# MLP's first product by seven block products in a phase of its own, its result by way of DRAM: a fused S5 and MLP layer on one core

## The chip, the cores and the metric

The kernel runs on 1 core of one Trainium2 chip. The metric is the time of the program on the device in microseconds, the median of several runs. TensorE (PE) multiplies and writes to PSUM, which has 8 banks of 128x512 float32; VectorE (DVE), ScalarE (ACT) and GpSimd (POOL) work element by element; SyncE (SP) only issues transfers. SBUF holds 128 partitions.

## The reference

One layer over 1024 latent tokens of width 1024, with a short context. A diagonal state-space mixer (S5) comes first, then a squared-ReLU MLP of width 4096, each behind a modulated RMS norm:

```python
def _mlp(h, w1, b1, w2, b2):
    a = jax.nn.relu(h @ w1 + b1)
    return (a * a) @ w2 + b2
...
x = x + g1 * y            # y: S5, GELU, then z * sigmoid(z @ glu_w + glu_b)
x = x + g2 * _mlp(_modulate(_rmsnorm(x, norm2_g[i]), sh2, sc2),
                  mlp_w1[i], mlp_b1[i], mlp_w2[i], mlp_b2[i])
...
return _rmsnorm(x, final_g)
```

All is float32: w1 is 1024 x 4096, w2 4096 x 1024.

## The kernel before

Activations are held transposed: channels on partitions (8 tiles of 128, index `d` or `k`), tokens along the row, in two halves of 512 (`halves[0]`, `halves[1]`, index `hf`). A float32 operand of a product is split into a high half, which the format of TensorE holds exactly, and a low half, what is left of it. ACT makes the high half by a cast, DVE or POOL subtracts it from the source. `mm3` then multiplies high by high, high by low and low by high: three matmuls of 128x128 weights with a 128x512 operand.

The kernel has a fixed order: `tc.manual_schedule()` leaves every engine's instructions in the order in which the code names them, and each engine takes them one after the other. Waits between engines are put in where data demand them.

The stages that matter here come last. The S5 part ends at about 370 us. Then follows the gate `z @ glu_w` (matmuls of `gate`, results of `gate_out`): sigmoid on ACT, two operations on DVE, into the residual `acc`. `z_sum` on POOL adds the two halves of z again. `sum_sq` collects the sum of squares of `acc`, `norm_cols` and `norm_rows` turn it into a factor per token by small matmuls, and `norm2` writes the normalised and modulated activations, split, over z (`zt(k)`). This is done for the first half of the tokens, then for the second.

The MLP runs over 16 blocks `b` of 256 hidden units. Block b takes the columns 256b to 256b+255 of w1 (1 MB, `load_w1`) and the same rows of w2 (1 MB, `load_w2`). For each block and token half, `m1_` makes two hidden tiles `f` of 128 (24 matmuls each, over 8 `k`), relu and square on ACT, split into the tiles A or GW. `m2_` multiplies them by w2 (48 matmuls), and DVE adds each of the 8 results, times g2, to `acc` (L1089). Nothing between the two products leaves SBUF. The list `order` sets the turn of blocks and halves: `m1_` of one entry stands ahead of `m2_` of the entry before. The weights of the next block are split behind that (`next_w1`, `next_w2`), into regions of the tile W that alternate. Raw weights have two buffers, w1 in UT from block 2 on and w2 in T.

The last block's second half is cut into two pieces of 256 tokens, so that the final norm of the first half and the stores run beside it.

Of the kernel before, what the change touches and what calls it, by code (L numbers as in the profile page):

```python
# [47 lines left out]
def kernel(ctx, tc, cst, bc, x, xl, ada_w, glu_w, w1, w2, out):  # L48
# [16 lines left out]
    KD = dp.tile([8, 128 * 1024], F32, name="KD")  # L65

# [823 lines left out]
    ring = [[sb(10240 + 512 * i, 512) for i in range(3)] + [at(UT, 512 * i, 512) for i in range(4)]]  # L890
    nt = [0]

    def tmp():
        nt[0] += 1
        return ring[0][nt[0] % len(ring[0])]
# [9 lines left out]
    def wpart(i):  # L905
        return at(W, 4096 * i, 4096)

    def raw1(b):
        return vw(raw[b > 1], 8, 256)

    def load_w1(b):
        SP.dma_start(out=raw1(b), in_=w1.rearrange("(k p) f -> p k f", p=128)[:, :, 256 * b:256 * b + 256])

    def load_w2(b):
        SP.dma_start(out=vw(raw[0], 2, 1024), in_=w2.rearrange("(k p) f -> p k f", p=128)[:, 2 * b:2 * b + 2])

    def w1s(b):
        return vw(wpart((3, 1)[b % 2]), 2, 8, 256)

    def w2s(b):  # L920
        return vw(wpart((0, 2)[b % 2]), 2, 2, 1024)

    def split_w1(b):
        split(w1s(b)[:, 0], w1s(b)[:, 1], raw1(b))

    def split_w2(b, eng=V):
        split(w2s(b)[:, 0], w2s(b)[:, 1], vw(raw[0], 2, 1024), eng)
# [92 lines left out]
    load_w1(0)  # L1020
# [10 lines left out]
    split_w1(0)  # L1031
    load_w1(1)
# [7 lines left out]
    for d, b in ((4, 6), (5, 7), (6, 1), (7, 3)):  # L1040
        for k in range(8):
            gate(bank(b), d, 1, k)
            if (d, k) == (4, 1):
                rb = norm_rows(r_, 2)
                for _ in norm2(range(8), 0, rb):
                    pass
                for e in range(2):
                    sum_sq(e, halves[1])
    gate_outs([(2, 4), (3, 5), (4, 6), (5, 7)], 1)
    w1_hi, w1_lo = w1s(1)[:, 0], w1s(1)[:, 1]  # L1050
    S.copy(w1_hi, raw1(1))
    gate_outs([(6, 1), (7, 3)], 1)
    V.tensor_tensor(w1_lo, raw1(1), w1_hi.bitcast(F32), op=OP.subtract)  # L1053
    load_w2(0)


    na = [0]

    def m1_mm(b, f, hf, ks=range(8)):
        o = bank((2, 0, 1, 3)[na[0] % 4])  # L1060
        w, fs = w1s(b), slice(128 * f, 128 * f + 128)
        for k in ks:
            z = zt(k)
            mm3(o, (w[:, 0, k, fs], w[:, 1, k, fs]), (z[:, 0, halves[hf]], z[:, 1, halves[hf]]), k == 0, k == 7)
        return o

    def m1_(b, f, hf):
        return m1_out(b, f, m1_mm(b, f, hf))

    def m1_out(b, f, o):  # L1070
        r = tmp()
        a = at(A, 1024 * (na[0] % 4), 2, 512) if na[0] % 4 < 3 else at(GW0, 0, 2, 512)
        na[0] += 1
        S.activation(r, o, AF.Relu, bias=C("b1")[:, 2 * b + f:2 * b + f + 1])  # L1074
        S.activation(r, r, AF.Square)
        split(a[:, 0], a[:, 1], r)
        return a

    def m2_(b, toks, ds, aa, o_=0):
        w = w2s(b)  # L1080
        n = toks.stop - toks.start
        ts = slice(o_, o_ + n)
        for f in range(2):
            for d in ds:
                ds_ = slice(128 * d, 128 * d + 128)
                mm3(bank(4 + d % 4, n), (w[:, 0, f, ds_], w[:, 1, f, ds_]), (aa[f][:, 0, ts], aa[f][:, 1, ts]), f == 0, f == 1)
# [22 lines left out]
    def next_w1(b):  # L1109
        split_w1(b)  # L1110
        if b < 15:
            load_w1(b + 1)

    def next_w2(b):
        split_w2(b)
        if b < 15:
            load_w2(b + 1)


    order = [(0, 0), (1, 0), (0, 1), (1, 1)] + [(b, hf) for b in range(2, 16) for hf in range(2)]  # L1120
    aa = {}
    for i, (b, hf) in enumerate(order[:-1]):
        if i == 1:
            oo = {}
            for n in range(16):
                if n == 3:
                    r_, *_ = norm_cols(7)
                elif n == 9:
                    rb = norm_rows(r_, 2)
                na[0] += n // 8  # L1130
                oo[n // 8] = m1_mm(1, n // 8, 0, [n % 8])
                na[0] -= n // 8
            n2 = norm2(range(8), 1, rb, P)
            for d in range(8):
                if d == 0:
                    split_w2(0, P)
                    load_w2(1)
                if d >= 5:
                    m2_(0, halves[0], [d - 5], aa[0, 0])
                next(n2, 0)  # L1140
            for _ in n2:
                pass
            ring[0] = ring[0][:3]
            load_w1(2)
            for d in range(8 - 5, 8):
                m2_(0, halves[0], [d], aa[0, 0])
            aa[1, 0] = [m1_out(1, f, oo[f]) for f in range(2)]
            next_w2(1)
        else:
            aa[b, hf] = [m1_(b, f, hf) for f in range(2)]  # L1150
        if b == 2:
            add_b2(hf)
        if i > 1:
            pb, ph = order[i - 1]
            for d in range(8):
                m2_(pb, halves[ph], [d], aa[pb, ph])
        if i == 2:
            next_w1(2)
        elif i == 3:
            next_w2(2)  # L1160
        elif b > 1 and hf == 0 and b < 15:
            next_w1(b + 1)
            next_w2(b + 1)


    first, toks = halves[0], (slice(512, 768), slice(768, 1024))
    m2_sq(15, first, range(5), aa[15, 0], eng=V)
    ab = [m1_(15, 0, 1)]
    o = m1_mm(15, 1, 1)
    m2_(15, first, [5], aa[15, 0])  # L1170
    sum_sq(4, first, V)
    ab.append(m1_out(15, 1, o))
    for d in range(6, 8):
        m2_(15, first, [d], aa[15, 0])
    for d in range(5, 8):
        sum_sq(d, first, V)
    m2_(15, toks[0], range(4), ab)
    n1 = norm_cols(1, first)
    r_ = next(n1)
    for d in range(8):  # L1180
        if d > 3:
            m2_(15, toks[0], [d], ab)
# [5 lines left out]
    for d in range(8):  # L1188
        m2_sq(15, toks[1], [d], ab, 256)
# [85 lines left out]
```

## Time and profile before

| what | value |
|---|---|
| median of 3 runs | 1155.51 us (1154.93 to 1155.67) |
| profiled execution, its own time | 1157.56 us |
| its span, first to last instruction | 1155.8 us |
| TensorE busy | 1020.3 us, 88% of the span |
| DVE busy | 706.2 us, 61% |
| ACT busy | 453.8 us, 39% |
| mean granted TensorE clock | 0.938 |

Busy time is a sum over stages with different limits, so it doesn't say by itself what bounds the kernel. The granted clock is that of TensorE, 1.00 for 2.4 GHz and 0.50 for 1.2 GHz. Matmuls overlap, so the distance between two starts is what one costs, not the time that a row gives for it.

### The profile page before, as it was taken

The page shows a single profiled execution, that of the slowest core. Times are in us where ns is not written, and L with a number is a line of the kernel's source. Part 1 is how long each engine was busy: PE and PEld are TensorE (multiplying, and loading weights), DVE is VectorE, ACT ScalarE, POOL GpSimd, SP SyncE. Part 2 cuts the span into 40 slices and gives each one's busy share as a digit, 9 for nine tenths or more (in the row PEclk, how much of TensorE's full clock was granted, in tenths as well). Part 3 has the DMA queues.
Part 4 walks back from the last instruction along what each step waited for, and adds up shares of the span by engine and source line. Part 5 has one row for each costly group of instructions (what it writes and reads, how often), then busy time and mean ns, then how long its engine had stood idle before and what let it go on. Part 6 is the DMA issues. An engine that isn't in the chain of part 4 may idle for free.

```text
span 1155.8 us, 14432 instructions
## 1 busy us (share of the span) xinstructions
PE 1020.3 (88%) x5584; PEld 845.4 (73%) x5584; DVE 706.2 (61%) x1093; ACT 453.8 (39%) x784; POOL 306.4 (27%) x240
## 2 busy tenths in 40 slices
PE   3569685555989898999999999999999999999995
PEld 3348564434878786888888888888888888888885
DVE  8998998999956775544354354354354354354347
ACT  7148574237873455625423223223223223223223
POOL 2876999615563735300000000000000000000003
PEclk9779888766999898999999999999999999999998
DMA  9414355494768102213021021021021021020004
GB/s 375 164 46 152 120 161 142 79 262 141 233 222 279 63 19 73 73 37 105 5 73 64 10 73 60 14 73 55 19 73 50 24 73 43 30 73 1 1 1 146
DMA packets 57477, 107.18 MB, mean 93 GB/s; under 512 B 3648, under 2 KB 39488, under 8 KB 56256
## 3 DMA queue, kind: packets, MB, share of 16 engines
q1 hardware_dynamic: 52976, 91.58, 24.2%
q10 hardware_dynamic: 4432, 14.68, 3.8%
q8 instruction: 44, 0.72, 0.3%
q14 instruction: 25, 0.20, 0.1%
HBM read 88.42 MB, written 17.83 MB: 92 GB/s over the span
## 4 chain that ended last, share of the span: by engine, by line
PE 64%; DVE 23%; ACT 4%; DMA 3%; issue 3%; POOL 1%; SPq 1%; DVEq 0%; POOLq 0%; ACTq 0%
PE PS L770 20%; PE PS L772 20%; PE PS L771 20%; DVE X L467 2%; DVE X L466 2%; DVE PS L465 2%; DVE PS L464 2%; DVE X L448 1%; DMA DY<-X 1%; DVE PS L697 1%; DVE T L940 1%; DVE UT L699 1%; ACT T L722 1%; SPq L582 1%; DMA T<-DY 1%
## 5 line engine op out<-in xcount | busy, mean ns | idle before, releaser
L1089 DVE SCALAR_TENSOR_TENSOR T<-PS,T 128x512 f32<-128x512 f32 (+1 forms) x264 | 190.6, 733 | 102.5 <-PE PS L772 101.7
L772 PE MATMUL PS<-z,W 128*128 128x512 f32 x608 | 238.9, 393 | 5.7 <-DVE W L1053 5.7
L770 PE MATMUL PS<-z,W 128*128 128x512 f32 x608 | 239.4, 394 | 0.0
L771 PE MATMUL PS<-z,W 128*128 128x512 f32 x608 | 238.7, 393 | 0.0
L955 POOL TENSOR_TENSOR T<-T 128x256 f32<-128x256 f32 x14 | 10.3, 735 | 664.3 <-ACT T L954 663.7
L1074 ACT ACTIVATE T<-PS,T 128x512 f32<-128x512 f32 x63 | 43.5, 690 | 358.4 <-PE PS L772 358.4
L94 DVE TENSOR_TENSOR A<-T,A 128x512 fp32r<-128x512 f32 x47 | 32.5, 692 | 206.6 <-ACT A L93 206.6
L770 PE MATMUL PS<-A,W 128*128 128x512 f32 (+1 forms) x392 | 151.1, 385 | 0.0
L771 PE MATMUL PS<-A,W 128*128 128x512 f32 (+1 forms) x392 | 150.8, 385 | 0.0
L772 PE MATMUL PS<-A,W 128*128 128x512 f32 (+1 forms) x392 | 150.8, 385 | 0.0
L772 PEld LDWEIGHTS PS<-z,W 128*128 128x128 f32 x608 | 115.6, 190 | 30.4 <-DVE W L1053 6.1
L771 PEld LDWEIGHTS PS<-z,W 128*128 128x128 f32 x608 | 115.6, 190 | 24.0
L770 PEld LDWEIGHTS PS<-z,W 128*128 128x128 f32 x608 | 115.6, 190 | 24.0
L771 PEld LDWEIGHTS PS<-A,W 128*128 128x128 f32 x392 | 73.6, 188 | 14.7
L770 PEld LDWEIGHTS PS<-A,W 128*128 128x128 f32 x392 | 73.6, 188 | 14.7
L772 PEld LDWEIGHTS PS<-A,W 128*128 128x128 f32 x392 | 73.6, 188 | 14.6
L486 PE MATMUL PS<-X,E 128*64 128x160 f32 x256 | 51.0, 341 | 27.5 <-DVE X L448 17.9
L93 ACT CAST W<-T 128x2048 fp32r<-128x2048 f32 x17 | 32.5, 1914 | 92.5 <-PE PS L771 92.5
L486 PEld LDWEIGHTS PS<-X,E 128*64 128x64 f32 x256 | 35.2, 154 | 38.6 <-issue 22.8
L487 PE MATMUL PS<-X,E 128*64 128x128 f32 x256 | 54.6, 320 | 0.0
L94 DVE TENSOR_TENSOR GW<-T,GW 128x512 fp32r<-128x512 f32 x16 | 11.1, 692 | 66.4 <-ACT GW L93 66.4
L771 PE MATMUL PS<-GW,W 128*128 128x512 f32 (+1 forms) x136 | 51.2, 376 | 0.0
(254 smaller groups left out, 1881.2 us busy)
## 6 DMA issues: line engine op xcount, KB each, us to landing
T<-in_w_dram SPq DMA_DIRECT2D x18, 1024.0 KB, 6.1
UT<-in_w_dram SPq DMA_DIRECT2D x14, 1024.0 KB, 5.3
T<-in_ada_w_dram ACTq DMA_DIRECT2D x17, 512.0 KB, 4.0
X<-in_x_dram SPq DMA_DIRECT2D x8, 640.0 KB, 10.0
DX<-X SPq DMA_DIRECT2D x8, 640.0 KB, 3.2
T<-DX SPq DMA_DIRECT2D x8, 640.0 KB, 5.1
T<-in_ada_w_dram SPq DMA_DIRECT2D x9, 512.0 KB, 5.3
X<-in_ada_w_dram SPq DMA_DIRECT2D x4, 1024.0 KB, 14.9
```

The lines of the kernel that those rows point to most:

```text
L93: S.copy(hi, src)
L94: eng.tensor_tensor(lo, src, hi.bitcast(F32), op=OP.subtract)
L464: ops = [lambda: eng.tensor_tensor(ta, src, lr, op=OP.mult), lambda: eng.tensor_tensor(tb_, src[:, :, ::-1], li, op=OP.mult), lambda: eng. ...
L465: lambda: eng.tensor_tensor(tb_, src[:, :, ::-1], li, op=OP.mult),
L466: lambda: eng.tensor_tensor(out_, out_, ta, op=OP.add),
L486: PE.matmul(b[0:64, c], e[:, g, c, 0:64], uj[:, g], start=True, stop=True)
L487: PE.matmul(b[64:128, c, :, 16:80], e[:, g, c, 64:128], uj[:, g, ::-1, 16:80][:, :, ::-1], start=True, stop=True)
L770: PE.matmul(o, wt[0], xt[0], start=start, stop=False)
L771: PE.matmul(o, wt[0], xt[1], start=False, stop=False)
L772: PE.matmul(o, wt[1], xt[0], start=False, stop=stop)
L1074: S.activation(r, o, AF.Relu, bias=C("b1")[:, 2 * b + f:2 * b + f + 1])
L1089: V.scalar_tensor_tensor(o, bank(4 + d % 4, n), g2[:, d:d + 1], o, op0=OP.mult, op1=OP.add)
```

## The change

The MLP is cut into two phases. In phase 1 all of `z @ w1` is made, 16 slices of 256 columns. A slice is a 2 x 2 block matrix: two halves of the contraction (`kh`, four k each) by two tiles `f` of 128 columns; z is one of two contraction halves by two token halves. Strassen's algorithm (in Winograd's form) makes the four results from seven block products of four k each, instead of eight:

- The seven right operands `zop` are the four blocks of z, partly overwritten, and three sums of them, t1, t2 and t4. They are made once. Differences of z are formed on TensorE, by products with the identity and its negative (`z_diff`), the others on DVE, with the first half's normalised x written to DRAM (XD, in `norm2`) and read back (`load_bf`).
- The seven left operands are made for each slice: `prep1` subtracts or adds blocks of the raw slice, partly in place, and splits the result into one of eight `slot`s. `prep(p + 6)` is called behind product p.
- `after1` adds the seven results up to four (`pu`, `pv`, `p12`, `p11`, in `places` of 128x512), then relu, square and a store to YD in DRAM.

The order `L` takes the products 0 and 5 of the slices 0, 1 and 2 first, which need the first token half alone; the other five of each follow, then all seven of the slices 3 to 15. Weights of products up to p = 15 are split by POOL, the others by DVE. There is one raw buffer of 1 MB for w1; the load of the next slice stands behind the split of a22 (product 6).

In phase 2 the rows of y are read back and split (`load_y`, `put_y`), and multiplied by w2 for two blocks at a time (`UNITS`), accumulated in one bank over both, so DVE adds half as many results to `acc`. `start2` puts the first two splits of w2 and the first loads of y into the last slice of phase 1. The last block stands apart and keeps the tail of before.

Ahead of the MLP, `gate_out` leaves the sigmoid and its product with z in PSUM instead of SBUF, the first w1 loads take half slices, split ahead of time (`put_w1_half`), and the last two sums of squares go from POOL to DVE. The addition of g2*b2 goes from ACT to POOL.

```diff
     def gate_out(b, d, hf):
-        sg, zz = tmp(), zf[d, hf]
         o = acc[:, d, halves[hf]]
-        S.activation(sg, b, AF.Sigmoid, bias=C("glub")[:, d:d + 1])
-        V.tensor_tensor(zz, zz, sg, op=OP.mult)
-        V.scalar_tensor_tensor(o, zz, g1[:, d:d + 1], o, op0=OP.mult, op1=OP.add)
+        S.activation(b, b, AF.Sigmoid, bias=C("glub")[:, d:d + 1])
+        V.tensor_tensor(b, zf[d, hf], b, op=OP.mult)
+        V.scalar_tensor_tensor(o, b, g1[:, d:d + 1], o, op0=OP.mult, op1=OP.add)
...
+    def put(to, src, eng=V, *dims):
+        hi, lo = (vw(v[:, 0:size(dims)], *dims) for v in to) if dims else to
+        S.copy(hi, src)
+        eng.tensor_tensor(lo, src, hi.bitcast(F32), op=OP.subtract)
...
+    def prep1(p, eng=V):
+
+        b, i = L[p]
+        to = slot(p)
+        w = vw(raw[0], 2, 4, 256)
+        a11, a12, a21, a22 = (w[:, kh, :, 128 * f:128 * f + 128] for f in range(2) for kh in range(2))
+        if i in (0, 5, 6):
+            put(to, (a11, a12, a22)[(0, 5, 6).index(i)], eng, 4, 128)
+            if i == 6:
+                load_w1(b + 1) if b < 15 else load_w2(0)
+            return
+        o = at(G2, 0, 4, 128) if i == 3 else a21
+        eng.tensor_tensor(o, *((a21, a22), (a21, a11), (a12, a21), (a22, a21))[i - 1], op=(OP.add, OP.subtract)[i > 1])
+        put(to, o, eng, 4, 128)
+
+    def product1(p):
+        b, i = L[p]
+        hi, lo = (vw(v, 4, 128) for v in slot(p))
+        for k in range(4):
+            mm3(pbank(p), (hi[:, k], lo[:, k]), zop[i][k], k == 0, k == 3)
...
+    def y_out(y, b, f, hf):
+        S.activation(y, y, AF.Relu, bias=C("b1")[:, 2 * b + f:2 * b + f + 1])
+        S.activation(y, y, AF.Square)
+        SP.dma_start(out=y_dram(b, f, hf), in_=y)
...
+        if i == 0:
+            S.copy(p11, o)
+        elif i == 2:
+            add(pu, p11)
+            V.tensor_tensor(pv, pu, pbank(p - 1), op=OP.add)
+        elif i == 3:
+            add(p12, pv)
+            y_out(p12, b, 0, 1)
+        elif i == 4:
+            add(pv, pv)
+            add(pu, pu)
+            y_out(pv, b, 1, 1)
+        elif i == 5:
+            add(y11, p11)
+            y_out(y11, b, 0, 0)
+        elif i == 6:
+            add(pu, pu)
+            y_out(pu, b, 1, 0)
...
+    def start2(i):
+
+        if i == 1:
+            load_w2(1)
+        if i in (2, 3):
+            put_w2(0, i - 2)
+        if i in (4, 5):
+            put_w2(1, i - 4)
+        if i == 4:
+            load_y(0, range(4))
+        if i == 6:
+            put_y(0, range(4))
+            load_y(0, range(4, 8))
...
+    ring = places[:5]
+    for p in range(6):
+        if p == 5:
+            norm2_second(range(4))
+            for k in range(4):
+                z_diff(k, zop[4][k], zop[0][k])
+            norm2_second(range(4, 8))
+            for k in range(4):
+                put(t1[k], sums[k])
+        product1(p)
+        after1(p)
+        prep(p + 6)
+        if p == 1:
+            r_, *_ = norm_cols(7)
+        elif p == 3:
+            rb = norm_rows(r_, 1)
...
+    for k in range(4):
+        z_diff(k, zop[3][k], zop[4][k])
+        load_bf(k)
+        V.tensor_tensor(bf[k], bf[k], sums[k], op=OP.add)
+        put(t2[k], bf[k])
+    product1(6)
+    after1(6)
+    prep(12)
+    for k in range(4):
+        put(zop[4][k], sums[k])
+        load_bf(4 + k)
+        V.tensor_tensor(bf[4 + k], bf[4 + k], bf[k], op=OP.subtract)
+        put(t4[k], bf[4 + k])
+    for p in range(7, len(L)):
+        b, i = L[p]
+        product1(p)
+        after1(p)
+        prep(p + 6)
+        if b == 15:
+            start2(i)
+        if i == 6 and 2 < b < 11:
+            P.tensor_scalar(acc[:, b - 3], acc[:, b - 3], g2b2[:, b - 3:b - 2], None, op0=OP.add)
```

Three places in the order of instructions follow, as the built program has them. First POOL at the start of phase 1. L1105 is the sum or difference of `prep1`, L919 the low half of `put`, L1022 the low halves that `norm2` writes for the second token half (z tiles); A, W and G_2904 are slots and scratch, T the raw slice.

```order
L1105 TENSOR_TENSOR T<-T 128x4x128
L919 TENSOR_TENSOR A<-T,A 128x512
L1105 TENSOR_TENSOR T<-T 128x4x128
L919 TENSOR_TENSOR A<-T,W 128x512
L1105 TENSOR_TENSOR G_2904<-T 128x512
L919 TENSOR_TENSOR W<-G_2904,W 128x512
L1105 TENSOR_TENSOR T<-T 128x4x128
L919 TENSOR_TENSOR W<-T,W 128x512 x2
L1022 TENSOR_TENSOR z_2289<-UT,z_2289 128x512
L1022 TENSOR_TENSOR z_2340<-T,z_2340 128x512
```

Before, POOL had one split of 128x2048 (w2) ahead of those low halves; now nine operations for five products stand there.

Second, DVE within one slice of phase 1. L1134 and L1139 are the adds of `after1`, reading PSUM (PS); L1105 and L919 are as above.

```order
L1134 TENSOR_TENSOR T<-T,PS 128x512
L1139 TENSOR_TENSOR T<-T,PS 128x512
L1105 TENSOR_TENSOR T<-T 128x4x128
L919 TENSOR_TENSOR W<-T,W 128x512
L1134 TENSOR_TENSOR UT<-T,PS 128x512
L1105 TENSOR_TENSOR T<-T 128x4x128
L919 TENSOR_TENSOR A<-T,A 128x512
L1134 TENSOR_TENSOR T<-T,PS 128x512 x2
```

Before, DVE had eight additions L1089 in a row here, between splits of whole slices (128x2048).

ACT at the same place, from the first product of a slice on: L1136 is the copy of p11, L918 the high half of `put`, L1118 relu, L1119 square.

```order
L1136 COPY T<-PS 128x512
L918 CAST W<-T 128x512
L918 CAST A<-T 128x512 x2
L1118 ACTIVATE UT<-UT,T 128x512
L1119 ACTIVATE UT<-UT 128x512
L918 CAST A<-T 128x512
```

Before, ACT had a relu, a square and a cast of the result itself for every 24 matmuls; now a cast of the next weights stands behind each relu and square, three more times in a slice.

Third, SP's queue in phase 1: L924 loads a w1 slice, L1120 stores a tile of y.

```order
L924 DMA T<-in_w_dram 128x8x256
L1120 DMA YD<-UT 128x512
L1120 DMA YD<-T 128x512 x3
L924 DMA T<-in_w_dram 128x8x256
L1120 DMA YD<-UT 128x512 x4
```

Before, the queue held a load of w1 and one of w2 in turn, into different buffers, and no store.

## Rows read from the trace of the kernel before

**Rows 1.** The page: span, and busy time of each engine.

```profile
span 1155.8 us, 14432 instructions
PE 1020.3 (88%) x5584; PEld 845.4 (73%) x5584; DVE 706.2 (61%) x1093; ACT 453.8 (39%) x784; POOL 306.4 (27%) x240
```

**Rows 2.** A window: length; busy us of PE, PEld, DVE, ACT, POOL; clock; DMA.

```profile
500.00:600.00 100.00, 100.00 (x442) 82.78 (x442) 44.14 (x51) 38.71 (x51) 0.00 (x0) 1.00 0.18 63
```

**Rows 3.** Timeline of SP: start, length, two loads of w1 in a row.

```profile
542.21 0.37 SPq L912 DMA_DIRECT2D UT<-in_w_dram  x1
...
585.73 0.37 SPq L912 DMA_DIRECT2D UT<-in_w_dram  x1
```

**Rows 4.** Timeline of PE at the first stop, and a window behind it.

```profile
393.57 0.39 PE L772 MATMUL PS<-z,W 128*128 128x512 f32 x1
398.12 1.86 PE L976 MATMUL PS<-T,UT 128*128 128x1 f32 x8 [4.15 <-POOL UT L955]
400.41 0.63 PE L771 MATMUL PS<-z,W 128*128 128x512 f32 x1
400.84 0.63 PE L772 MATMUL PS<-z,W 128*128 128x512 f32 x1
407.52 1.05 PE L994 MATMUL PS<-T 128*128 128x128 f32 x8
399.00:404.00 5.00, 5.00 (x15) 4.13 (x16) 4.96 (x4) 1.54 (x2) 3.57 (x2) 0.50 0.25 60
```

**Rows 5.** The same at the second stop.

```profile
446.03 0.79 PE L772 MATMUL PS<-z,W 128*128 128x512 f32 x1 [5.69 <-DVE W L1053]
446.00:455.00 9.00, 8.97 (x25) 7.42 (x26) 3.11 (x7) 4.47 (x5) 2.92 (x2) 0.50 0.36 118
```

**Rows 6.** Timelines of POOL and DVE in the gate and the norm.

```profile
377.33 1.84 POOL L955 TENSOR_TENSOR UT<-UT,T 128x512 f32<-128x512 f32 x1 [5.93 <-ACT T L954]
...
438.77 1.76 DVE L940 TENSOR_TENSOR T<-T 128x512 f32<-128x512 f32 x1 [3.45 <-POOL T L934]
441.23 0.68 DVE L940 TENSOR_TENSOR T<-T,UT 128x512 f32<-128x512 f32 x1
465.10 0.68 DVE L1002 TENSOR_TENSOR T<-T,PS 128x512 f32<-128x512 f32 x1
463.62 5.07 POOL L1013 TENSOR_TENSOR z<-UT,z 128x512 fp32r<-128x512 f32 x4
```

**Rows 7.** Timeline of ACT in the MLP: relu, square, high half.

```profile
528.35 0.69 ACT L1074 ACTIVATE T<-PS,T 128x512 f32<-128x512 f32 x1 [3.43 <-PE PS L772]
529.08 0.63 ACT L1075 ACTIVATE T<-T 128x512 f32<-128x512 f32 x1
529.74 0.62 ACT L93 CAST A<-T 128x512 fp32r<-128x512 f32 x1
```

**Rows 8.** Timeline of DVE just behind: low half, and three waiting additions.

```profile
530.40 0.69 DVE L94 TENSOR_TENSOR A<-T,A 128x512 fp32r<-128x512 f32 x1 [4.75 <-ACT A L93]
531.01 2.18 DVE L1089 SCALAR_TENSOR_TENSOR T<-PS,T 128x512 f32<-128x512 f32 x3
```

**Rows 9.** Issue to landing: w1 loads (L912), w2 (L915), and two kinds from the page.

```profile
L912 SPq DMA_DIRECT2D UT<-in_w_dram x12: 367/368/368, 542.2 to 1020.9; - x12
DMA to landing us min/median/max: 5.2/5.3/5.6
L915 SPq DMA_DIRECT2D T<-in_w_dram x13: 368/368/368, 521.5 to 1023.1; - x13
DMA to landing us min/median/max: 5.1/6.3/7.5
T<-DY SPq DMA_DIRECT2D x8, 512.0 KB, 3.8
out_dram<-T SPq DMA_DIRECT2D x6, 256.0 KB, 2.3
```

**Rows 10.** Timeline of PE where the pieces of 256 tokens begin.

```profile
1126.55 0.28 PE L770 MATMUL PS<-A,W 128*128 128x256 f32 x1
```

More of the change, by code (lines that the diff above doesn't have):

```diff
@@ L889 @@
     ss = at(UT, 2048, 512)
-    ring = [[sb(10240 + 512 * i, 512) for i in range(3)] + [at(UT, 512 * i, 512) for i in range(4)]]
+    places = [sb(10240 + 512 * i, 512) for i in range(3)] + [at(UT, 512 * i, 512) for i in range(5)]
+    ring = places[:7]
     nt = [0]
@@ L894, in tmp @@
         nt[0] += 1
[L895 removed]
+        return ring[nt[0] % len(ring)]
     for d in range(8):
@@ L1048 @@
                     sum_sq(e, halves[1])
+                for kh in range(2):
+                    put_w1_half(2, kh, 4 + kh)
+                load_w1(0)
     gate_outs([(2, 4), (3, 5), (4, 6), (5, 7)], 1)
[L1050 to L1080, printed above, removed]
+    gate_outs([(6, 1), (7, 3)], 1, eng=V)
+    def zh(k, hf):
+        z = zt(k)
+        return z[:, 0, halves[hf]], z[:, 1, halves[hf]]
@@ new lines, with y_slot, w2_slot @@
+    UNITS = [[2 * u, 2 * u + 1] for u in range(7)] + [[14], [15]]
+    raw2 = raw[0], at(UT, 512, 2048)
+    def y_slot(u, j):
+        if u % 2 == 0:
+            t, o = (zs[j // 2], 1024 * (j % 2)) if j < 4 else (W, 8192 + 1024 * (j - 4))
+        else:
+            t, o = (zs[6 + j // 2], 1024 * (j % 2)) if j < 4 else (W, 12288 + 1024 * (j - 4))
+        return at(t, o, 512), at(t, o + 512, 512)
+    def w2_slot(u, pi):
+        if u % 2 == 0:
+            return [at(W, 4096 * pi + 2048 * n, 2, 1024) for n in range(2)]
+        return [at(zs[2 + 2 * pi + n], 0, 2, 1024) for n in range(2)]
@@ new lines, in ys_of, with load_y, put_y, load_w2 @@
+    def ys_of(u):
+        return [4 * hf + 2 * pi + f for hf in range(2) for pi in range(len(UNITS[u])) for f in range(2)]
+    def load_y(u, js):
+        for j in js:
+            hf, pi, f = j // 4, j // 2 % 2, j % 2
+            SP.dma_start(out=y_slot(u, j)[1].bitcast(F32), in_=y_dram(UNITS[u][pi], f, hf))
+    def put_y(u, js):
+        for j in js:
+            to = y_slot(u, j)
+            put(to, to[1].bitcast(F32))
+    def load_w2(b):
+        if b < 16:
+            SP.dma_start(out=vw(raw2[b % 2], 2, 1024), in_=w2.rearrange("(k p) c -> p k c", p=128)[:, 2 * b:2 * b + 2])
@@ new lines, in step2 @@
+    def step2(u, t):
+        v = u + 1
+        js = ys_of(v)
+        if t == 0:
+            load_y(v, js)
+        w = [(b, f) for b in UNITS[v] for f in range(2)]
+        at_ = {2 * n: (put_w2, *a) for n, a in enumerate(w)}
+        free = [n for n in range(3, 16) if n not in at_]
+        at_.update({n: (put_y, v, [j]) for n, j in zip(free, js)})
+        f, *a = at_.get(t, (None,))
+        if f:
+            f(*a)
+    unit = at(W, 11776, 2, 128)
+    sums = [bank(i) for i in (5, 7, 4, 6)]
@@ new lines, in z_diff, with norm2_second @@
+    def z_diff(k, a, b_):
+        mm = [(unit[:, 0], v) for v in a] + [(unit[:, 1], v) for v in b_]
+        for n, (w, v) in enumerate(mm):
+            PE.matmul(sums[k], w, v, start=n == 0, stop=n == 3)
+    def norm2_second(ks):
+        for _ in norm2(ks, 1, rb, P):
+            pass
+    S.copy(unit[:, 0], ident)
+    S.activation(unit[:, 1], ident, AF.Identity, scale=-1.0)
+    ring = places[:5]
[14 more added lines that the diff above has]
+            rb = norm_rows(r_, 1)
@@ L1081, in m2_ @@
+    first, toks = halves[0], (slice(512, 768), slice(768, 1024))
+    def m2_(toks, ds, aa, o_=0):
+        w = w2_slot(8, 0)
         n = toks.stop - toks.start
@@ L1107, in last @@
             store(d - 1, toks, SP)
[L1109 to L1177, printed above, removed]
+    ring = ring[:3]
+    aa, ab = ([y_slot(8, 4 * hf + f) for f in range(2)] for hf in range(2))
+    m2_sq(first, range(8), aa, eng=V)
+    m2_(toks[0], range(4), ab)
     n1 = norm_cols(1, first)
```

106 lines of the change are left out of this document (81 added, 25 removed).

## The prediction

> **What bounds the kernel now.** I read the page's busy table first: TensorE works 88% of the span and no other engine over 61% [rows 1]. That share is an average, so the stretches come next. From 500 to 600 us, and likewise to 1100, TensorE is busy without a gap at full granted clock, with DVE busy 44% and ACT 39% of the time [rows 2]. The queue of SP confirms it from another side: w1 slices are fetched every 43.52 us [rows 3], and one slice is 192 matmuls of 512 columns (96 in each product of the MLP), so a matmul costs 43.52 / 192 = 0.2267 us. Fewer matmuls are worth 0.2267 us each as long as TensorE stays the one that is waited for. Ahead of that there are two stops. The first, of 4.15 us, is the wait for the sum of squares of the first half, after which matmuls start 0.43 us apart, at a granted clock of 0.50 (1.2 GHz) [rows 4]. The second, of 5.7 us, is for a weight split, again with a granted 0.50 behind it [rows 5].
>
> **What the change removes on TensorE.** A w1 slice takes 7 products of 12 matmuls, 84 instead of 96: 16 x 12 = 192 fewer; the differences of z cost 32 new ones. Net 160 x 0.2267 = 36.3 us less work. One product is 12 x 0.2267 = 2.72 us, a slice 19.04 us.
>
> **What it puts on the other engines.** In phase 1 DVE and ACT now run, step by step, what the second order fence shows: add, subtract, low half on DVE; relu, square, high half (cast) on ACT. Both take their instructions in order, and the low half of a weight waits for the cast that stands behind relu and square, which wait for the add. So a step is a chain across both engines, not two loads side by side. The trace has this chain: relu at 528.35, square 529.08, cast 529.74, low half on DVE 530.40, next DVE instruction 531.01 [rows 7, 8], 2.66 us, or 2.56 where the cast doesn't use the square's result and starts some 0.1 sooner. The add, a DVE operation on PSUM of 128x512, is 0.68 [rows 6], and 0.04 lies between engines. A step is 3.3 us, TensorE's product 2.72.
>
> A round (one slice, seven steps): five such steps (the first has two adds and no relu, 3.3 too) 16.5; then the step that copies p11 and splits a22, which adds 1.2 behind the fifth; then the load of the next slice, which may only start now, since there is one raw buffer and a22 is the last read of it: 5.3 to land [rows 9]; then cast and low half of the next a11, 0.62 + 0.04 + 0.61 = 1.3. Sum 24.3 us. DVE cannot fill the wait: the adds of the next step stand behind the low half that waits. Bounds: with landing 5.2 and steps of 3.2 it is 23.7; with landing 6.3, as the w2 loads have that share the queues [rows 9], and steps of 3.4, 25.8. The stores of y (256 KB, four a round) go just ahead of the load, so I don't go below the median.
>
> The Trainium skill gives 6.15 us for a transfer of 1 MB (DMA: Bandwidth & Descriptors, section Bandwidth); the trace has 5.3 for this very slice and the measurement decides. By the page the sum would be 12 x 0.85 = 10 us more, 1238.
>
> So in phase 1 a round takes 24.3 and not 19.0. Weights are prepared six products ahead, about 13 us of lead, but a lead is spent once and 5.3 are missing each round.
>
> **The path, against the times of the trace before.**
> (a) Gates. The sigmoid now stays in PSUM, and DVE's operations that read PSUM are not stretched by GpSimd: 0.68 beside GpSimd's 1.27 us operations, where the ones with both inputs in SBUF take 1.76 instead of 0.68 [rows 6]. GpSimd's eleven operations from 377.3 on then take 14, with some waits for squares to 392.5, and the sum of squares is there before TensorE asks for it at 393.8: the stop of 4.15 goes, the half clock behind it (12 matmuls at +0.2) and 0.6 on the slow column sums, 7.2; 0.9 come back, as the row sums wait for four weight splits put ahead of them on DVE. The gates end, 90 matmuls behind the row sums, at 422.4 instead of 428.7 (407.5 + 0.8 + 20.4 [rows 4]). Bounds: no gain (428.7), 7.2.
> (b) Start of phase 1. Two products, to 427.9; the second half's sum of squares is ready at 432.4 (GpSimd's eleven operations from about 415.5, 14, then two DVE operations, square and sum, 2.8): a stop of 4.5, half clock behind it; products 2 to 4 end at 445.4. The normalisation of the second half stands on GpSimd behind five weight preparations (nine operations of 1.3, each waiting for a cast in turn: first order fence), so its first low half comes at 451.3 (stop 5.9). Differences, product 5, second differences and product 6 end at 467.3. The operands t2, the new z and t4 go through one DVE-ACT chain of 2 us per k; reloads of x rows 5 to 7 each wait for a place in the ring of five, that is for the subtraction before, 0.4 issue and 2.6 landing (between 2.3 for a 256 KB store and 3.8 for a 512 KB load [rows 9]). Product 10 ends at 488.6 instead of the 462 that TensorE alone would need. From there the chain sets the pace: w1 slice 2 is asked for at 495, slice 3 at 519.3 (five steps, a landing, and some 4 us by which GpSimd's eight additions of g2b2, 128x1024 each, stretch DVE; no row has them, between 1 and 2.5 us each by GpSimd's neighbours of this kernel), slice 4 after one more 23 us at 542.3. Bounds: 15 less, 12 more.
> (c) Twelve rounds to the first w2 load: 12 x 24.3 = 291.6, to 833.9.
> (d) Hand-over. Four steps of slice 15 carry a split of w2 each (cast 1.0, low half 1.2, scaled from 128x2048), the first of them waits 5.6 for w2, and y is read back only then: ACT reaches the first y 22.2 behind that load's issue, its low half 23.5. TensorE has been out of products for 19 us. 857.4. Bounds 17 and 28.
> (e) Phase 2 without the last slice: 1440 matmuls, 326.4, and 4 for half clock after the stop (some 20 matmuls at +0.2, as behind 446.0 [rows 5]): 1187.8. DVE has half as many PSUM adds there and stays below TensorE.
> (f) The last slice's first half, 48 matmuls, 10.9: 1198.7.
> (g) The tail from the first 256-column matmul is the same code: 1155.8 - 1126.5 = 29.3 [rows 1, 10]. **Span 1228.0.** The profiled execution took 1157.6 for its span of 1155.8, the median of the runs is 1155.5; against the median the forecast is 1228.
>
> **The rivals.** *TensorE still sets the pace* (the other side). Then from product 10 on 101 x 2.72 = 274.7, a hand-over of some 3.5, then (e) to (g) without half clock: 488.6 + 274.7 + 3.5 + 326.4 + 10.9 + 29.3 = 1133. For it: DVE's own work is 18 operations of 0.6 to 0.7 a round, 12.4 of 19.0 us, and the share of busy time would call it free. It decides at a round of 19.0, that is exactly if the slice's landing did not stand in the chain. Against it: the one buffer, and the low half that holds the adds up. *TensorE falls to half clock for good in phase 1*, since it idles 5.3 of every 24.3 us: a slice is then 84 x 0.43 = 36 us, 12 x 11.7 = 140 more, 1368. Against it: the idle parts are five of about 0.6 and one of about 2.5, and the two stops with half clock behind them were 4.15 and 5.7 long [rows 4, 5]; a single drop costs nothing, as the products it delays stand ahead of the load's wait. The Trainium skill says that idle gaps between bursts put TensorE back to half clock (TensorE: Matmul & The Clock Gate, section HAM oscillation); the two stops agree, for gaps as short as here no row shows it. *Store and reload are hidden*: the hand-over costs 3.5 and not 23.5, since ACT isn't behind when phase 1 ends; 1204 and inside the range.
>
> **How the numbers follow.** Forecast (chain of DVE, ACT and load, 1228) 0.84; TensorE pace 0.10; half clock throughout 0.03; something between pace and chain (1140 to 1190) 0.03. Range: 12 rounds 23.7 to 25.8 is -7 to +18, (a) and (b) -15 to +18, (d) -6 to +5; they do not all fall one way, so 1195 to 1262, which the forecast fills with 0.95 of its chance. Changes under 0.2% (2.3 us) could not be told from none here: faster 0.12, same 0.02, slower 0.86.
>
> **What would show it.** Right: w1 loads 24 us apart in SP's queue from the fourth on; DVE's low halves (L919) waiting for ACT's casts and those for the DMA into T; TensorE idle by a fifth in phase 1 at full clock, ACT and DVE never caught up; a stop near 19 us at the hand-over; phase 2 gapless. Wrong: loads 19 us apart, or matmuls 0.43 us apart in phase 1. The forecast fails if casts or adds overtake what I hold to be one chain, or the first matmul of phase 2 comes within 10 us of the last product.

## The result, and the profile after

The changed kernel takes 1223.38 us, the median of 4 runs (1220.47 to 1223.69), against 1155.59 us for the kernel before, run beside it: a ratio of 1.058, 95% interval 1.0561 to 1.0598. It is 68 us slower; the forecast was 1228, 72 us slower. The profiled execution took 1223.68 us for a span of 1221.7.

The page of the kernel after, span and busy time (as [rows 1]):

```profile
span 1221.7 us, 14748 instructions
PE 1036.3 (85%) x5424; PEld 814.8 (67%) x5424; DVE 769.1 (63%) x1278; ACT 488.9 (40%) x914; POOL 340.3 (28%) x263
```

There are 160 matmuls fewer, as counted. No engine's share has risen much; from this view alone nothing is wrong. A window of phase 1 (as [rows 2]) shows more: 350 matmuls in 100 us instead of 442, at full granted clock, while DVE works 48 and ACT 41 of the 100 us. TensorE waits here for engines that are themselves idle half of the time.

```profile
600.00:700.00 100.00, 92.72 (x350) 61.43 (x348) 48.17 (x77) 40.67 (x67) 0.00 (x0) 1.00 0.25 86
```

SP's timeline, loads of w1 (L924) and the first load of w2 (L1186), as [rows 3]:

```profile
540.43 0.38 SPq L924 DMA_DIRECT2D T<-in_w_dram  x1
...
638.50 0.38 SPq L924 DMA_DIRECT2D T<-in_w_dram  x1
662.53 0.38 SPq L924 DMA_DIRECT2D T<-in_w_dram  x1
...
831.46 0.38 SPq L1186 DMA_DIRECT2D T<-in_w_dram  x1
```

A round, from one load of w1 to the next, takes 24.0 us here, and 291.0 / 12 = 24.25 in the mean (with one of 25.4, in which the landing took 6.7). Two timelines of one round show what it consists of: ACT first, then DVE, with the wait of each row in brackets.

```profile
643.85 0.62 ACT L918 CAST W<-T 128x512 fp32r<-128x512 f32 x1 [6.10 <-DMA T<-in_w_dram]
...
649.12 0.72 ACT L1118 ACTIVATE UT<-UT,T 128x512 f32<-128x512 f32 x1 [1.36 <-DVE UT L1134]
649.87 0.63 ACT L1119 ACTIVATE UT<-UT 128x512 f32<-128x512 f32 x1
650.41 0.60 ACT L918 CAST W<-T 128x512 fp32r<-128x512 f32 x1
```

```profile
644.50 0.69 DVE L919 TENSOR_TENSOR W<-T,W 128x512 fp32r<-128x512 f32 x1 [6.02 <-ACT W L918]
...
647.79 0.69 DVE L919 TENSOR_TENSOR W<-T,W 128x512 fp32r<-128x512 f32 x1 [0.69 <-ACT W L918]
648.40 0.68 DVE L1134 TENSOR_TENSOR UT<-T,PS 128x512 f32<-128x512 f32 x1
649.00 0.69 DVE L1105 TENSOR_TENSOR T<-T 128x512 f32<-128x512 f32 x1
651.05 0.69 DVE L919 TENSOR_TENSOR W<-T,W 128x512 fp32r<-128x512 f32 x1 [1.36 <-ACT W L918]
```

Read them together: the add at 648.40 releases the relu at 649.12, square and cast follow on ACT without a gap, the cast releases the low half at 651.05, and only behind it stands DVE's next add. In this step each engine waits 1.36 us for the other. From low half to low half a step is 3.26 us, and the landing of the slice adds one wait of 6.0 a round.

TensorE's timeline at the places of the path, as [rows 4, 5, 10]: the two norms, the differences of z (L1230), the hand-over, and the first matmul of 256 columns.

```profile
393.99 0.95 PE L979 MATMUL PS<-T,UT 128*128 128x1 f32 x8
...
433.69 1.86 PE L979 MATMUL PS<-T,UT 128*128 128x1 f32 x8 [4.74 <-DVE UT L958]
...
450.44 0.80 PE L1230 MATMUL PS<-z,W 128*128 128x512 f32 x1 [3.98 <-ACT z L1019]
...
835.38 0.39 PE L774 MATMUL PS<-W,A 128*128 128x512 f32 x1
853.86 0.80 PE L772 MATMUL PS<-z,W 128*128 128x512 f32 x1 [18.09 <-ACT z L918]
...
1193.74 0.28 PE L772 MATMUL PS<-W 128*128 128x256 f32 x1
```

L979 are the column sums of a norm. The first stop, 4.15 us in [rows 4], is gone; one of 4.74 stands at the second norm; the hand-over stops TensorE for 18.09 us. Behind it phase 2 runs without a gap up to the tail (busy 310 of 310 us from 880 on).

### The profile page after: what moved, and what is told of

The parts are those of the page before. It is cut to its first block, busy times and chain, and to the rows that moved or that the text cites. A ratio compares the mean times of both kernels' runs of the same rounds, so it can differ in the third digit from the quotient of the medians.

```text
span 1221.7 us, 14748 instructions
## 1 busy us (share of the span) xinstructions
PE 1036.3 (85%) x5424; PEld 814.8 (67%) x5424; DVE 769.1 (63%) x1278; ACT 488.9 (40%) x914; POOL 340.3 (28%) x263
## 4 chain that ended last, share of the span: by engine, by line
PE 31%; DVE 28%; ACT 14%; DMA 12%; issue 9%; POOL 4%; SPq 1%; DVEq 0%; ACTq 0%; POOLq 0%
PE PS L772 10%; PE PS L774 10%; PE PS L773 10%; DMA T<-in_w_dram 7%; ACT W L918 3%; DVE X L469 2%; DVE W L919 2%; DVE UT L1134 2%; ACT UT L1118 2%; ACT A L918 2%; DMA DY<-X 2%; DVE A L919 2%; DVE T L1134 2%; DVE X L468 2%; ACT T L1118 1%
## 5 line engine op out<-in xcount | busy, mean ns | idle before, releaser
L1297 DVE SCALAR_TENSOR_TENSOR T<-PS,T 128x512 f32<-128x512 f32 x128 | 96.1, 751 | 164.3 <-PE PS L774 164.3
L772 PE MATMUL PS<-z,W 128*128 128x512 f32 x400 | 164.6, 412 | 35.5 <-ACT z L918 19.8
L773 PE MATMUL PS<-z,W 128*128 128x512 f32 x400 | 161.4, 403 | 0.3 <-DVE z L919 0.3
L774 PE MATMUL PS<-z,W 128*128 128x512 f32 x372 | 151.9, 408 | 0.0
L918 ACT CAST W<-T 128x512 fp32r<-128x512 f32 (+1 forms) x73 | 47.6, 660 | 200.4 <-PE PS L773 101.0
L772 PEld LDWEIGHTS PS<-z,W 128*128 128x128 f32 x400 | 77.8, 195 | 62.0 <-ACT W L918 27.2
L772 PE MATMUL PS<-W 128*128 128x512 f32 (+1 forms) x280 | 109.0, 389 | 2.5 <-ACT W L918 2.4
L773 PE MATMUL PS<-W 128*128 128x512 f32 (+1 forms) x280 | 107.7, 385 | 0.2 <-DVE W L919 0.2
L919 DVE TENSOR_TENSOR W<-T,W 128x512 fp32r<-128x512 f32 (+1 forms) x58 | 47.3, 820 | 92.5 <-ACT W L918 92.5
L774 PE MATMUL PS<-W 128*128 128x512 f32 (+1 forms) x252 | 96.3, 382 | 0.0
L774 PEld LDWEIGHTS PS<-z,W 128*128 128x128 f32 x372 | 72.7, 195 | 25.6 <-DVE W L919 10.1
L773 PEld LDWEIGHTS PS<-z,W 128*128 128x128 f32 x400 | 78.0, 195 | 17.2 <-DVE z L919 1.5
L772 PEld LDWEIGHTS PS<-W 128*128 128x128 f32 x280 | 53.5, 191 | 18.1 <-ACT W L918 9.1
L919 DVE TENSOR_TENSOR A<-T,A 128x512 fp32r<-128x512 f32 x32 | 23.9, 748 | 60.5 <-ACT A L918 60.5
L773 PEld LDWEIGHTS PS<-W 128*128 128x128 f32 x280 | 53.4, 191 | 11.4 <-DVE W L919 1.9
L774 PEld LDWEIGHTS PS<-W 128*128 128x128 f32 x252 | 47.7, 189 | 12.2 <-DVE W L919 3.7
L774 PE MATMUL PS<-z,A 128*128 128x512 f32 x124 | 53.0, 428 | 0.0
L918 ACT CAST z<-T 128x1024 fp32r<-128x1024 f32 x8 | 8.1, 1050 | 106.4 <-PE PS L773 106.4
```

Source lines behind the costliest of these rows:

```text
L772: PE.matmul(o, wt[0], xt[0], start=start, stop=False)
L773: PE.matmul(o, wt[0], xt[1], start=False, stop=False)
L774: PE.matmul(o, wt[1], xt[0], start=False, stop=stop)
L918: S.copy(hi, src)
L919: eng.tensor_tensor(lo, src, hi.bitcast(F32), op=OP.subtract)
L1297: V.scalar_tensor_tensor(o, bank(t % 8), g2[:, d:d + 1], o, op0=OP.mult, op1=OP.add)
```

## The experiments

Theory: in phase 1 DVE, ACT and the landing of the next slice form one chain in series, five steps of 3.3 and a landing of 5.3, which is longer than TensorE's 19.04 us a round. Rivals: the steps alone bound it and the landing is covered by the six products of lead; or the landing alone, and the order in a step is innocent; or ACT, idle for 60%, has no part in it. The kernel before, run beside each group of experiments, took 1153.5 to 1154.9 us, so a difference of 1 or 2 us between versions of different groups says nothing.

**four_loads**: the slice in four loads, each behind the last read of its quarter.

```diff
-            if i == 6:
-                load_w1(b + 1) if b < 15 else load_w2(0)
+            next_w1(b, i, w)
...
+                if i == ((2, 5 if b > 2 else 3), (4, 6))[f][kh]:
+                    SP.dma_start(out=w[:, kh, :, 128 * f:128 * f + 128], ...)
```

> The next w1 slice comes in four loads of 256 KB, each issued behind the last read of its quarter of the raw buffer, so that the landing leaves the chain. Theory (one chain of DVE, ACT and load): a round of the chain falls from 24.15 us by about 6.1 to 18.0, under TensorE's 19.04, so TensorE sets the pace, ACT has caught up at the hand-over and its stop falls from 18.1 to some 4; 1145 to 1165 us. Rival (the steps alone bound the round, the landing is covered by six products of lead): 1215 or more. Rival (the queue is what is short): four smaller loads make it slower than 1223.

1159.39 us, ratio to before 1.0037 (1.0024 to 1.0051): 64 us less than the changed kernel. The rival of covered landings falls, and so does that of a short queue. Two numbers in the expectation were off. A round is 19.4 us, not 18.0, because the first sum of a slice still waits for its last quarter (SP's timeline, the load of one and the same quarter in two slices; DVE's timeline), and as the chain is still just longer than 19.04, ACT has not caught up and the hand-over stays at 18 us (TensorE's timeline).

```profile
636.89 0.39 SPq L1116 DMA_DIRECT2D T<-in_w_dram  x1
...
656.35 0.39 SPq L1116 DMA_DIRECT2D T<-in_w_dram  x1
```

```profile
651.80 0.69 DVE L1104 TENSOR_TENSOR T<-T 128x512 f32<-128x512 f32 x1 [1.44 <-DMA T<-in_w_dram]
```

```profile
787.35 0.80 PE L772 MATMUL PS<-z,W 128*128 128x512 f32 x1 [18.13 <-ACT z L918]
```

**reorder**: one load as before; the order in a step is sum, cast, additions, low half, relu, square.

```diff
         product1(p)
+        late[0] = []
+        prep(p + 6)
+        lows = late[0]
         after1(p)
-        prep(p + 6)
+        late[0] = None
+        for go in lows + outs:
+            go()
+        outs.clear()
+        if p + 6 < len(L):
+            loads(p + 6)
```

Here `put` only casts and leaves its low half in `late`, `y_out` leaves relu, square and store in `outs`, and `loads` asks for the next slice behind them.

> One load as before, but within a step the sum of the weights and its high half stand ahead of the additions of the result, the low half behind them, and relu and square last. Theory: a step falls from 3.26 us to about 2.05 (sum 0.69, cast 0.62, low half 0.69), the landing of 5.5 stays, a round of the chain is about 18.5, just under 19.04; 1150 to 1170 us. Rival (the landing alone is missing in each round, the order within a step costs nothing): 1215 to 1225.

1159.59 us, ratio 1.0041 (1.0024 to 1.0058). The landing alone is not to blame either: with the landing untouched, a shorter step wins back 64 us. Steps are 1.8 to 2.5 us, the six between two landings 12.7 together, and from the last low half before a landing to the first behind it 6.8 pass; the round is 19.6 (SP's timeline), 1.1 more than expected.

```profile
610.31 0.38 SPq L932 DMA_DIRECT2D T<-in_w_dram  x1
629.88 0.38 SPq L932 DMA_DIRECT2D T<-in_w_dram  x1
```

**both**: both edits.

> Both edits. Theory: the rounds are TensorE's 19.04 us already with either, so nothing is added there; only the first rounds, where the chain is still behind, gain: 1140 to 1160 us. If the two gains add up in full instead (twice what either gives), neither had reached TensorE's pace and the theory's arithmetic is wrong.

1141.25 us, ratio 0.9885 (0.9859 to 0.9911). The gains do not add (64 and 64 give 82): one edit brings the round close to TensorE's pace, the other takes off what was left, the hand-over above all (18.1 to 7.2 us). The expectation was right in its range and wrong in its reason: neither edit alone had brought the rounds to 19.04. A window shows phase 1 as [rows 2] showed the kernel before, without a gap, and TensorE's timeline the stop at the hand-over.

```profile
500.00:745.00 245.00, 245.00 (x1082) 202.86 (x1082) 159.25 (x243) 131.00 (x211) 17.56 (x6) 1.00 0.36 113
```

```profile
772.15 0.80 PE L772 MATMUL PS<-z,W 128*128 128x512 f32 x1 [7.19 <-ACT z L920]
```

**no_square**: the changed kernel without the square.

```diff
         S.activation(y, y, AF.Relu, bias=C("b1")[:, 2 * b + f:2 * b + f + 1])
-        S.activation(y, y, AF.Square)
```

> Leaves out the square behind relu in phase 1 (y is stored without it). Theory: each of the four squares of a round is 0.54 us of the chain, a round is 24.15 - 2.15 = 22.0, twelve rounds give 26 us: 1190 to 1200 us. Rival (ACT is busy for 40% of phase 1 and waits for most of it, so a shorter ACT changes nothing): 1220 to 1224.

1193.72 us, ratio 1.0334 (1.0295 to 1.0372), 30 us less than the changed kernel. An engine with 60% of its time idle was shortened by some 35 us of work (64 squares of 0.54), and 30 of that came off the total. A round is 22.4 us (SP's timeline), 22.5 in the mean; 12 x 1.75 = 21 comes from rounds, the rest from the start and the hand-over. The expectation had 22.0: three of the four steps with a square fall to 2.65 us, but the one with two additions stays at 3.26 (DVE's timeline), since there two additions, the sum and its cast take that long without the square.

```profile
648.85 0.38 SPq L924 DMA_DIRECT2D T<-in_w_dram  x1
671.25 0.38 SPq L924 DMA_DIRECT2D T<-in_w_dram  x1
```

**hand_over**: `both`, and in the last slice `start2(i)` is called between `prep` and `after1`, so that the splits of w2 fall under the same order.

```diff
         prep(p + 6)
+        if b == 15:
+            start2(i)
         lows = late[0]
...
-        if b == 15:
-            start2(i)
```

In `put_w2` the load that follows a split moves behind its low half as well.

> The version with four loads and the new order in a step, and in the last slice of phase 1 the splits of w2 in that order too: high half first, low half behind the additions, relu and square last. Theory (the stop at the hand-over is the chain of DVE and ACT over four steps of 4.2 us, not the way of y through DRAM): steps of about 2.5 us, the stop falls from 7.2 to 1 or 2 us and most of the 2 us of half clock behind it go: 6 to 8 us less than that version, 1133 to 1136. Rival (the reload of y is what it waits for): the first cast of y waits for its DMA, and the stop stays above 5 us.

1131.75 us, ratio 0.9793 (0.9759 to 0.9827): the best version, 1.2 below the range. The stop is now 0.90 us, and the first cast of y waits 0.79 for its reload (TensorE's and ACT's timelines). So of 18 us of hand-over 17 were ACT and DVE in series, taken off in two parts by `both` and this run, and the wait for y by way of DRAM is under 1.

```profile
764.43 0.50 PE L772 MATMUL PS<-z,W 128*128 128x512 f32 x1 [0.90 <-ACT z L920]
```

```profile
763.76 2.69 ACT L920 CAST z<-z 128x512 fp32r<-128x512 f32 x4 [0.79 <-DMA z<-YD]
```

**gate_only**: the kernel before, with the changed `gate_out` alone (its three lines in the diff of the change).

> The kernel before, with one part of the change: the sigmoid and its product with z stay in PSUM. Theory (DVE's operations with both inputs in SBUF are stretched by GpSimd's, 0.68 to 1.76 us; with one in PSUM they are not): the stop of 4.15 us for the sum of squares and the half clock behind it go, 5.3 us at the end of the gates as in the changed kernel, and the second stop, a weight split on DVE behind eight stretched operations, shrinks by up to 5.7 and 4 of half clock, less some 3 if GpSimd's second sum is late then: 1140 to 1152 us. Rival (the stops only move to the next wait): 1153 to 1156.

1137.56 us, ratio 0.9843 (0.9817 to 0.9869): 17 us faster than before, without any block product, and below the range I gave. The line of the product with z shows why: 16 operations, none above 0.70 us, where [rows 6] has 1.76. GpSimd's sums of squares beside them are shorter too, 1.29 us for the first (its timeline) where [rows 6] has 1.84.

```profile
L939 DVE TENSOR_TENSOR PS<-T,PS x8: 680/690/697, 370.6 to 424.8; 128x512 f32<-128x512 f32 x8
L939 DVE TENSOR_TENSOR PS<-UT,PS x8: 684/696/697, 373.4 to 418.2; 128x512 f32<-128x512 f32 x8
```

```profile
374.25 1.29 POOL L954 TENSOR_TENSOR UT<-UT 128x512 f32<-128x512 f32 x1 [8.08 <-ACT UT L953]
```

Both stops of [rows 4, 5], 4.15 and 5.69, and the half clock behind each are gone, with one wait of 0.24 us left up to the tail. The 3 us that I had set aside for a late GpSimd sum did not come. The edit also does without the temporary in SBUF that each sigmoid wrote; in the kernel before, one sigmoid waits 2.83 us for DVE's L941 (ACT's timeline, 381.52). How much of the 17 us is such a place that came free late, and how much the stretch itself, no run here separates.

**gate_old**: the changed kernel with the gate of before.

> The changed kernel with the old gate: sigmoid and its product with z in SBUF. Theory (GpSimd stretches DVE there; what it costs is paid in full, since phase 1 starts from the gates): the first stop is back, 5 us at the end of the gates, and the second half's sum of squares is later by its own stretched operations, another 1 to 8: 1229 to 1237 us. Rival (the start of phase 1 waits for other things, the GpSimd queue and the reloads of x): under 3 us, 1222 to 1226.

1233.2 us, ratio 1.0681 (1.0654 to 1.0709), 10 us more than the changed kernel, as the theory had it. TensorE's timeline has both prices: the first stop back, and the second up from 4.74 to 11.40.

```profile
394.73 1.87 PE L980 MATMUL PS<-T,UT 128*128 128x1 f32 x8 [4.15 <-POOL UT L959]
...
441.79 1.87 PE L980 MATMUL PS<-T,UT 128*128 128x1 f32 x8 [11.40 <-DVE UT L959]
```

The last four start from `hand_over` and ask what holds the start of phase 1 up. **norm_dve**: `norm2_second` with its low halves on DVE.

> The one before this, with the low halves of the second half's normalised z on DVE instead of GpSimd. Theory (they stand behind nine GpSimd operations of weight preparation): the stop of 3.94 and 0.56 us ahead of the differences of z goes, and with it some 2 us of half clock; DVE has room there: 4 to 6 us less. Rival (the high halves on ACT are late, or the DVE chain of the differences is next): less than 2 us.

1134.4 us, ratio 0.9819 (0.9789 to 0.9849): no gain. The stop was not GpSimd's. It waits for ACT's high half, and a second one comes up for the split of t1 on DVE (TensorE's timeline):

```profile
445.38 6.47 PE L1265 MATMUL PS<-z,W 128*128 128x512 f32 x16 [4.24 <-ACT z L1027]
457.74 5.34 PE L1265 MATMUL PS<-z,W 128*128 128x512 f32 x16 [3.17 <-DVE W L923]
```

**prep_dve**: all preparations on DVE (`prep1(p)` without the choice of POOL).

> The best version so far, with all weight preparations on DVE, so that nothing of them stands on GpSimd ahead of the second half's low halves. Theory (GpSimd's 1.3 us each, and ACT's casts that wait for them, hold the normalisation of the second half back): the stop of 4.0 and 0.55 us shrinks by 2 to 4 and with it some half clock: 1126 to 1130 us. Rival (the DVE queue, which waits for the store of a y tile just ahead of the normalisation, holds it back): less than 2 us, 1130 to 1134.

1140.91 us, ratio 0.9882 (0.9857 to 0.9908), 9 us worse than `hand_over`. GpSimd, free early, takes its eight additions of g2b2 from 460 on (its timeline), beside DVE's chain of t2 and t4, where low halves go from 0.69 to up to 1.53 us (DVE's timeline). Neither theory had that.

```profile
460.16 22.61 POOL L1324 TENSOR_SCALAR T<-T 128x1024 f32<-128x1024 f32 x8
```

```profile
474.40 1.53 DVE L923 TENSOR_TENSOR W<-T,W 128x512 fp32r<-128x512 f32 x1 [0.69 <-ACT W L920]
477.23 1.53 DVE L923 TENSOR_TENSOR A<-T,A 128x512 fp32r<-128x512 f32 x1 [0.69 <-ACT A L920]
...
492.48 0.69 DVE L923 TENSOR_TENSOR W<-UT,W 128x512 fp32r<-128x512 f32 x1 [0.68 <-ACT W L920]
```

It is only part of the loss. The last row is the last low half of t4, and `hand_over` has it 7.5 us sooner, as much as lies between the spans of the two profiled executions:

```profile
484.93 0.69 DVE L923 TENSOR_TENSOR W<-UT,W 128x512 fp32r<-128x512 f32 x1 [0.69 <-ACT W L920]
```

The stretch of DVE's operations in the chain is some 3 of that. A weight's preparation that GpSimd did now stands in the chain itself (its low half is the row at 477.23), 2.0 without its stretch. The rest lies for the most part ahead of the chain, where the stop for ACT's high half is 5.02 instead of 3.99.

**y11_place**: another place for the first tile of y.

```diff
-            p11, y11 = places[5 + b], at(G2, 512, 512)
+            p11, y11 = places[5 + b], places[7] if b == 0 else at(G2, 512, 512)
```

> The version with the hand-over in order, with another place for the first tile of y, so that the addition of product (1, 5) need not wait for its store. Theory (that addition, 3.7 us behind the store, holds DVE's normalisation and ACT's casts of weights, and so the high half of the second half's z): ACT's normalisation starts 1 to 2 us sooner, the stop ahead of the differences of z falls from 4.0 to 2 or 3: 1129 to 1131 us. Rival (GpSimd's preparation, which ACT's casts wait for in turn, is the next to be late): the stop stays at 4.0.

1131.99 us, ratio 0.9819 (0.9789 to 0.9848), 1 above the range. In DVE's timeline of the changed kernel the addition of product (1, 5) waits 3.57 us for the store of the one place that the tiles of the first slices have, and DVE's normalisation stands behind it:

```profile
444.84 0.69 DVE L1134 TENSOR_TENSOR G<-UT,PS 128x512 f32<-128x512 f32 x1 [3.57 <-DMA YD<-G]
445.44 0.68 DVE L1009 TENSOR_TENSOR UT<-T,PS 128x512 f32<-128x512 f32 x1
```

With two places TensorE's stop is 3.12 instead of the 3.99 of `hand_over`, so the wait was real, but 0.9 us is less than this comparison can tell in the total.

**norm_first**: normalisation of four tiles ahead of two steps of preparation.

```diff
         if p == 5:
-            norm2_second(range(4))
...
         product1(p)
+        if p == 3:
+            rb = norm_rows(r_, 1)
+            norm2_second(range(4))
         after1(p)
         prep(p + 6)
...
-        elif p == 3:
-            rb = norm_rows(r_, 1)
```

> The same version, with the normalisation of four tiles of the second half ahead of the two steps of weight preparation that stood before it. Theory (it is the place in ACT's order, behind two casts of weights, that makes the high halves late; GpSimd's low halves follow at once): the stop of 4.0 and 0.55 us goes and with it some 2 us of half clock: 1125 to 1129 us. Rival (the prepared weights are late instead): a new wait of products on weights behind the differences, and 1130 or more.

1133.39 us, ratio 0.9832 (0.9807 to 0.9857): the rival's outcome, though the new wait is not for a prepared weight. The wait for ACT's high half is gone (0.85 is GpSimd's), and 5.29 stand 13 us later, for the split of t1, with the two steps and the rest of the normalisation now ahead of it:

```profile
446.14 4.73 PE L1265 MATMUL PS<-z,W 128*128 128x512 f32 x15 [0.85 <-POOL z L1030]
...
458.90 6.62 PE L1265 MATMUL PS<-z,W 128*128 128x512 f32 x16 [5.29 <-DVE W L923]
```

## Why the prediction was right, and where it was off

| step | forecast, us | measured |
|---|---|---|
| (a) gates end | 422.4 | 423.4 (24 matmuls before 428.8) |
| (b) load of slice 4 | 542.3 | 540.4 |
| (c) twelve rounds | 291.6 | 291.0 |
| (d) hand-over, from the first load of w2 | 23.5 | 22.4 |
| (e) and (f) phase 2 to the tail | 341.3 | 339.9 |
| (g) tail | 29.3 | 28.0 |
| span | 1228.0 | 1221.7 |

**The central step held, by its mechanism.** Phase 1 was forecast as one chain of steps of 3.3 us with a landing of 5.3 in it. The trace has 3.26 and 5.35 (638.50 to the cast at 643.85). The landing taken out, the steps shortened, and one link taken away gave 64, 64 and 30 us, which no rival allows. The prediction also named the point of decision, a round of 19.04: with 19.4 the hand-over still cost 18 us, with 19.6 still 16 (`reorder`), and only with 19.04, in `both`, did it fall to 7.

**Half clock for good did not come.** That rival was priced at 140 us and 0.03. In the twelve rounds TensorE stops once a round, for the landing. Behind six of these stops the matmuls go on 0.23 us apart, behind the other six they are 0.43 apart for some ten matmuls, and the length of the stop does not tell which. Two rounds, each with the stop and a window around it (as [rows 2], the clock third from the end):

```profile
692.84 0.50 PE L772 MATMUL PS<-z,A 128*128 128x512 f32 x1 [1.92 <-ACT A L918]
688.00:700.00 12.00, 10.07 (x39) 6.55 (x37) 5.10 (x9) 3.10 (x5) 0.00 (x0) 1.00 0.29 93
...
789.27 0.50 PE L772 MATMUL PS<-z,W 128*128 128x512 f32 x1 [1.72 <-ACT W L918]
784.00:796.00 12.00, 10.29 (x37) 7.76 (x36) 4.66 (x8) 3.10 (x5) 0.00 (x0) 0.86 0.29 90
```

The round takes 24.25 us at the first place and 24.07 at the second (SP's timeline): the products that the slow clock delays stand ahead of a wait. The Trainium skill says that idle gaps between bursts put TensorE back to half clock (TensorE: Matmul & The Clock Gate, HAM oscillation). Six of these stops bear that out in kind; as a price it is nothing in these rounds.

**Terms that were mis-sized.** In (b), the additions of g2b2 were given some 4 us of stretch, and between 1 and 2.5 us each. They took 24.3 us for eight, 3.0 each (GpSimd's timeline), but beside them three of four sums with both inputs in SBUF stretched, to 1.33 us in the mean (DVE's groups from 500 to 520 us), which is 3 x 0.64 = 1.9; the low halves, which also read SBUF alone, stayed at 0.69 and the adds from PSUM at 0.68. So this term was 2.1 too large. From the load of slice 2 to that of slice 3 21.6 us passed and not 24.3; slice 2 was 0.7 late and the round behind slice 3 0.2 longer, which makes the 1.9 by which (b) was too late.

```profile
L1105 DVE TENSOR_TENSOR T<-T 128x512 f32<-128x512 f32 x3 | 4.0, 1326 | 8.8 <-DMA T<-in_w_dram 8.8
L1134 DVE TENSOR_TENSOR UT<-UT,PS 128x512 f32<-128x512 f32 x4 | 2.6, 681 | 0.0
L919 DVE TENSOR_TENSOR W<-T,W 128x512 fp32r<-128x512 f32 x3 | 2.1, 692 | 2.5 <-ACT W L918 2.5
```

In (a) I took 0.9 for the row sums' wait; it was 1.4, half of what (a) was too early by. Step (d) was 1.1 too long, inside its bounds. (e) had 4 us for half clock behind the hand-over; ten matmuls were slow there and cost 2.6 (TensorE's timeline), which is the 1.4 of (e) and (f). (g) was 1.3 too long, and why the tail is shorter no run shows. From (b) on all the errors fall one way, and together they are the 6.3 us by which the span was forecast too long.

**A step that was right by number and wrong by reason.** In (b) the differences of z were to wait for GpSimd's low halves behind five preparations, a stop of 5.9 ending at 451.3. GpSimd began the first low half at 450.5, and TensorE had it at 451.8 after stops of 3.98 and 0.56. But the 3.98 are for ACT's high half, which comes late by its place in ACT's order (the wait goes in `norm_first`), 0.9 of it by the store in `y11_place`; GpSimd's part is 0.56. That the end came so near to the forecast is luck. Moving single pieces (`norm_dve`, `y11_place`, `norm_first`) moved the wait and gained nothing; which order would be best for the start of phase 1 stays open.

**What the change is worth in its parts.** The gate alone gives 17 us. All the rest of the change, the block products above all, then loses 1223.4 - 1137.6 = 86 as written. In the best version it gains 5.8 by the medians, though the intervals of the two ratios still overlap. Of 36.3 us of saved matmuls nearly all the rest went into the start of phase 1, by an estimate from these windows. In the same 70 us `hand_over` runs 207 matmuls and `gate_only` 318 (windows of both kernels), 111 x 0.2267 = 25.2 us; about 3 us of the stop at the second norm lie ahead of this window, 0.9 more at the row sums and 1.1 at the hand-over, which leaves 6.

```profile
430.00:500.00 70.00, 59.27 (x207) 44.07 (x208) 33.08 (x52) 37.03 (x64) 40.20 (x28) 0.80 0.27 83
```

```profile
430.00:500.00 70.00, 70.00 (x318) 58.21 (x317) 35.00 (x48) 31.87 (x43) 15.04 (x10) 1.00 0.24 76
```

## What to carry to other kernels

Where two engines hand results to each other within every step and take instructions in order, add the step up as a chain and compare it with the step of the engine that should set the pace; busy shares of 48% and 41% said nothing here. A single buffer puts the whole landing into that chain once a round, and either freeing it piece by piece or putting what the next step needs (the sum and its high half) ahead of the results that go out (relu, square, store) won back 64 of the 68 us lost. Test the small edits that come along with a large one by themselves: three lines in the gate were worth three times what all the rest brought in the best version.

## What was not expected of the hardware

DVE's operations with both inputs in SBUF took up to 1.3 to 1.8 us beside GpSimd's instead of 0.69, those with one input in PSUM 0.68 to 0.70. The Trainium skill (SBUF — State Buffer, SBUF: two separate sides) tells of a pair of ports that GpSimd and a DVE operation with two SBUF inputs take by turns, each for a whole instruction; the row of 1.76 agrees, being 0.68 and 1.1 of a GpSimd operation of 1.27; the low halves that kept 0.69 beside the additions of g2b2 show that not every such operation is held up. The forecast used the rows, but not how far they reach: putting the sigmoid's result in PSUM removed two stops and the half clock behind both, 17 us, and moving work off GpSimd made the kernel 9 us slower, in part since what GpSimd did next then stood beside DVE's SBUF operations. Loads of w1 in quarters, with rows half as long, did not show as a cost: the phase ran without a gap.
